# RMS norm and matmul on one core: x held in two buffers of sixteen tiles instead of five of eight

## The chip, the cores and the metric

The kernel runs on one core of a Trainium2 chip. The metric is the device time of one execution in microseconds; of several executions the median is given. One execution was also recorded by the hardware profiler, and all lines in profile fences come from that record or from questions put to its trace.

## The reference

x has 16 x 1024 rows of 512 numbers. Each row is divided by the root of the mean of its squares, scaled by gamma, and multiplied by a 512 x 768 weight matrix, all in float32:

```python
rms = np.sqrt(np.mean(x ** 2, axis=-1, keepdims=True) + eps)
x_norm = x / rms * gamma
return np.matmul(x_norm, weight).astype(np.float32)
```

x is 33.6 MB, the output 50.3 MB, the weights 1.6 MB.

## The kernel before

The 16384 rows are 128 tiles of 128 rows. Two tiles make a pair, and the main loop runs over the pairs j = 2 to 63; the first four tiles are written out by hand before it. Gamma is folded into the weights once, and the division by the root is left to the end, as a factor of each output row.

A tile goes through these steps. A DMA from SP's queue loads x (`load`, L82). GpSimd (POOL) casts a pair to bf16 (`cast`, L93, into `xb`, four buffers). ACT squares each tile with a sum along the row (`square`, L97, which also reads x) and takes the root (L101); DVE takes the reciprocal (L103). TensorE (PE) transposes the cast pair in four pieces, two bf16 numbers at a time as one float32 word (L120, into `tp`), and DVE moves the pair from PSUM to SBUF (`evac`, L127, into `xT`). Eight matmuls a tile follow (L155, into an accumulator `ops`, three buffers). ACT finishes the even tiles (L137) and DVE the odd ones (L139), each into the output buffer `ot`, and SP's queue stores it (`store`, L152).

The order of every engine's instructions is that of the program text. In iteration j POOL is told to cast pair j+3, ACT to square pair j+1, and a feeder puts the four transposes of pair j+2 between the matmuls of pair j. Since POOL has nothing else to do, it casts as soon as an `xb` buffer is free, which is when PE has transposed the pair four before.

x lies in SBUF in groups of G = 8 tiles, each in one of five buffers of 16 KB per partition. The first group is loaded in pieces of 1, 2, 1, 2 and 2 tiles, the second in two of 4, and each later group by one DMA of 2 MB in which a partition takes eight rows that lie together. Before the loop the loads of tiles 0 to 31 are issued (`load_until(AHEAD)`, with the weights between the first three tiles and the rest). In iteration j, `load_until(2 * j + AHEAD)` with AHEAD = 28 issues each group whose first tile is under 2j + 28; a group's buffer is that of the group five before.

The output lies in groups of eight tiles as well, in three buffers of 24 KB per partition. A group's store is issued after its last tile; the first group and the last two are stored in pieces.

All loads of x and all stores go through SP, which issues them in the order of the program and waits before each for its data or its buffer.

Of the kernel before, what the change touches and what calls it, by code (L numbers as in the profile page):

```python
# [12 lines left out]
F32 = mybir.dt.float32  # L13
BF16 = mybir.dt.bfloat16
AF = mybir.ActivationFunctionType
# [3 lines left out]
def kernel(  # L19
# [8 lines left out]
    nc = tc.nc  # L28
    P = 128

    x = x.flatten_outer_dims()
    out = out.flatten_outer_dims()
    N, D = x.shape
    _, O = out.shape
    K = D // P
    NT = N // P
    NP = NT // 2
    G = 8
    NG = NT // G
    AHEAD = 28  # L40
    WIDE = 512

    def stretches(parts):
        first, size, i = {}, {}, 0
        for g in range(NG):
            for n in parts.get(g, [G]):
                for t in range(i, i + n):  # L50
                    first[t], size[t] = i, n
                i += n
        return first, size

    opening = [1, 2, 1, 2, 2]
    x_first, x_size = stretches({0: opening, 1: [4, 4]})
    o_first, o_size = stretches({0: opening, NG - 2: [4, 4], NG - 1: [2, 2, 2, 1, 1]})

    def rows(ap, i, n):
        if i < G:  # L60
            return ap[i * P:(i + n) * P, :].rearrange("(p t) d -> p t d", t=n)
        return ap.rearrange("(g p t) d -> g p t d", p=P, t=G)[i // G, :, i % G:i % G + n, :]

    singles = ctx.enter_context(tc.tile_pool(name="singles", bufs=1))
    xin = ctx.enter_context(tc.tile_pool(name="xin", bufs=5))
    xbp = ctx.enter_context(tc.tile_pool(name="xb", bufs=4))
    junk = ctx.enter_context(tc.tile_pool(name="junk", bufs=2))
    stats = ctx.enter_context(tc.tile_pool(name="stats", bufs=4))
# [3 lines left out]
    outp = ctx.enter_context(tc.tile_pool(name="out", bufs=3))  # L72

    x_tiles, xb_tiles, tp_tiles, rstd_of, xT_tiles, o_tiles = {}, {}, {}, {}, {}, {}

    def held(tiles, i, n=1):
        return tiles[i // G][:, i % G:i % G + n, :]

    def load(i):
        if i // G not in x_tiles:  # L80
            x_tiles[i // G] = xin.tile([P, G, D], F32, name="xt")
        nc.sync.dma_start(out=held(x_tiles, i, x_size[i]), in_=rows(x, i, x_size[i]))  # L82

    starts = [i for i in range(NT) if x_first[i] == i]

    def load_until(i):
        while starts and starts[0] < i:
            load(starts.pop(0))

    def cast(i, engine, n=1):  # L90
        if i // 2 not in xb_tiles:
            xb_tiles[i // 2] = xbp.tile([P, 2, D], BF16, name="xb")
        engine.tensor_copy(out=xb_tiles[i // 2][:, i % 2:i % 2 + n, :], in_=held(x_tiles, i, n))  # L93

    def square(i, ssq):
        jk = junk.tile([P, D], BF16, name="jk")
        nc.scalar.activation(out=jk, in_=held(x_tiles, i)[:, 0, :], func=AF.Square, accum_out=ssq)  # L97

    def root(i, n, ssq):
        rms = stats.tile([P, 4], F32, name="rms")  # L100
# [29 lines left out]
    def transpose_tile(i):  # L130
        for h in range(2):
            transpose_word(i // 2, i % 2, h)
        evac(i // 2, i % 2, 1)

    def scale(engine, dst, src, r):
        if engine is nc.scalar:
            nc.scalar.mul(out=dst, in_=src, mul=r)  # L137
        else:
            nc.vector.tensor_single_scalar(out=dst, in_=src, scalar=r, op=mybir.AluOpType.mult)  # L139

    def accumulator():
        return opsum.tile([P, 2, WIDE], F32, name="ops").rearrange("p a b -> p (a b)")

    def out_tile(i):
        if i // G not in o_tiles:
            o_tiles[i // G] = outp.tile([P, G, O], F32, name="ot")
        return o_tiles[i // G][:, i % G, :]

    def store(i):
        first, n = o_first[i], o_size[i]  # L150
        if i == first + n - 1:
            nc.sync.dma_start(out=rows(out, first, n), in_=held(o_tiles, first, n))  # L152

    def matmul(i, k, acc, lo, hi):
        nc.tensor.matmul(out=acc[:, lo:hi], lhsT=xT_tiles[i // 2][:, i % 2, k // 2, :, k % 2], rhs=w_bf[:, k, lo:hi],  # L155
# [3 lines left out]
    def matmuls(i, acc, ks, feed=None):  # L159
        for k in ks:  # L160
            matmul(i, k, acc, 0, WIDE)
            if feed:
                feed()
            matmul(i, k, acc, WIDE, O)
# [20 lines left out]
    with tc.manual_schedule():  # L185
        g_row = singles.tile([2, P, 2], F32)
        nc.scalar.dma_start(out=g_row, in_=gamma.rearrange("(h w c) -> h w c", w=P, c=2))

        wv = weight.rearrange("(h w c) o -> w h (c o)", w=P, c=2)
        touched = singles.tile([P, 2, 1], F32)  # L190
        nc.scalar.dma_start(out=touched, in_=wv[:, :, 0:1])
        nc.scalar.preload_act_table(AF.Sqrt)  # L192
        load_until(3)
        w_f32 = singles.tile([P, K, O], F32)
        for h in range(2):
            nc.sync.dma_start(out=w_f32[:, 2 * h:2 * h + 2, :].rearrange("p c o -> p (c o)"), in_=wv[:, h, :])
        load_until(AHEAD)


        warm = singles.tile([P, WIDE], BF16)  # L200
        nc.vector.memset(warm, 0.0)  # L201
        eps_sb = singles.tile([P, 1], F32)
        nc.vector.memset(eps_sb, float(eps))  # L203
        ident_f = singles.tile([P, P], F32)
        make_identity(nc, ident_f)
        spare = accumulator()

        def warm_up(n):
            for _ in range(n):
                nc.tensor.matmul(out=spare[:, :WIDE], lhsT=warm[:, :P], rhs=warm, start=True, stop=True)  # L210

        w_bf = singles.tile([P, K, O], BF16)

        def weights(k, engine, lo=0, hi=O):
            scale(engine, w_bf[:, k, lo:hi], w_f32[:, k, lo:hi], g_sb[:, k % 2, k // 2:k // 2 + 1])


        ssq = stats.tile([P, 4], F32, name="ssq")
        warm_up(6)
        cast(0, nc.vector)  # L220
        square(0, ssq[:, 0:1])
        gp = tpsum.tile([P, 2, 2], F32, name="tp")
        for c in range(2):
            nc.tensor.transpose(out=gp[:, c, :], in_=g_row[:, :, c], identity=ident_f[:2, :2])  # L224
        g_sb = singles.tile([P, 2, 2], F32)
        nc.vector.tensor_copy(out=g_sb, in_=gp)  # L226
        transpose_tile(0)
        warm_up(3)
        cast(1, nc.vector)
        cast(2, nc.gpsimd)  # L230
        square(1, ssq[:, 1:2])
        square(2, ssq[:, 2:3])
        transpose_tile(1)
        transpose_tile(2)
        warm_up(2)

        acc = [accumulator() for _ in range(4)]
        weights(0, nc.vector, 0, WIDE)
        weights(0, nc.vector, WIDE, O)
        weights(1, nc.scalar)  # L240
        for k in (0, 1):
            for i in range(3):
                matmuls(i, acc[i], [k])
        root(0, 3, ssq)
        weights(2, nc.vector)
        weights(3, nc.scalar)
        cast(3, nc.gpsimd)
        matmuls(0, acc[0], [2, 3])
        finish_tile(0, acc[0], nc.scalar)
        transpose_tile(3)  # L250
        norms(3, 1)
        matmuls(1, acc[1], [2, 3])
        finish_tile(1, acc[1], nc.vector)
        cast(4, nc.gpsimd)
        cast(5, nc.gpsimd)
        matmuls(2, acc[2], [2, 3])
        finish_tile(2, acc[2], nc.scalar)
        matmuls(3, acc[3], [0, 1, 2, 3], feeder([2], [0, 2, 2, 0], alone=True))
        finish_tile(3, acc[3], nc.vector)
        cast(6, nc.gpsimd, 2)  # L260
        cast(8, nc.gpsimd, 2)
        norms(4, 2)


        one, two, both = [1, 1, 0, 1, 1, 0, 0, 0], [1, 0, 1, 0, 1, 0, 1, 0], [1, 1, 1, 1, 1, 1, 1, 1]
        for j in range(2, NP):
            load_until(2 * j + AHEAD)
            if j + 3 < NP:
                cast(2 * j + 6, nc.gpsimd, 2)
            if j + 1 < NP:  # L270
                norms(2 * j + 2, 2)
            if j == NP - 1:
                break
            if j < 4:
                feed = feeder([j + 1], one)
            elif j == 4:
                feed = feeder([5, 6], both)
            elif j + 2 < NP:
                feed = feeder([j + 2], two)
            else:  # L280
                feed = None
            for i, engine in ((2 * j, nc.scalar), (2 * j + 1, nc.vector)):
                a = accumulator()
                matmuls(i, a, range(K), feed)
                finish_tile(i, a, engine)


        for i in (NT - 2, NT - 1):
            for lo, hi, engine in ((0, WIDE, nc.scalar), (WIDE, O, nc.vector)):
                a = accumulator()  # L290
                for k in range(K):
                    matmul(i, k, a, lo, hi)
                scale(engine, out_tile(i)[:, lo:hi], a[:, lo:hi], rstd_of[i])
            store(i)
# [35 lines left out]
```

## Time and profile before

| | |
|---|---|
| median of 12 runs | 211.21 us (210.99 to 211.59) |
| the profiled execution's own time | 211.21 us |
| its span in the profile | 209.4 us |
| bytes moved by DMA | 85.69 MB, mean 409 GB/s |
| x loads: whole groups, issue to landing | 14 of 2048 KB, median 24.6 us |
| stores: whole groups, issue to landing | 13 of 3072 KB, median 20.1 us |
| granted clock of TensorE, mean | 0.992 |

The span begins with the first recorded instruction and ends with the last; about 1.8 us of the execution's time lie around it. PE is the TensorE matmul, DVE is VectorE, ACT is ScalarE, POOL is GpSimd, SP the engine that issues the DMAs here. In a row of slices each digit is the busy share of a fortieth of the span in tenths. In a row of a group stand the line, the engine, the operation, what it writes and reads with the shape, how often, then its busy time and the mean of one in ns, and last the engine's idle time before it and what ended most of that. "Landing" is the time from the issue of a DMA to its last completion.

### The profile page before, as it was taken

Reading aid. Unit: us, or ns where it says so; the run is one execution under the profiler, and the core shown is the slowest. Engines: PE = TensorE matmul, PEld = TensorE weight load, DVE = VectorE, ACT = ScalarE, POOL = GpSimd, SP = SyncE. Lnnn points to the kernel's source line nnn. Section 1 sums busy time; section 2 is a strip of 40 time slices with the busy share of each in tenths; the row PEclk is TensorE's granted clock in tenths of the full one; section 3 lists DMA queues with packets and bytes.
Section 4 is the critical chain, followed back from the end, with each engine's and each line's share of the span. In section 5 each row is a group of like instructions: output and inputs, shape, how many; then the busy total and the mean of one; then the engine's idle time right before and its main releaser. Section 6 shows DMA issues by size and latency. Waiting matters only on the chain.

```text
span 209.4 us, 3580 instructions
## 1 busy us (share of the span) xinstructions
PE 199.6 (95%) x1293; PEld 137.4 (66%) x1293; DVE 111.7 (53%) x204; ACT 158.2 (76%) x388; POOL 66.3 (32%) x71
## 2 busy tenths in 40 slices
PE   7799999999999999999999999999999999999960
PEld 3466766776667766776666766677666776667630
DVE  2565664465456545644654565466456545644630
ACT  4599788778777877887787778778777877887830
POOL 1156443233233323332332333233323323310000
PEclk9999999999999999999999999999999999999996
DMA  6999999999999999999999999999999999998983
GB/s 220 406 430 438 376 406 412 429 448 408 437 441 412 440 415 441 412 438 429 418 448 407 443 408 444 435 415 438 412 448 424 419 444 421 418 432 366 396 363 135
DMA packets 7206, 85.69 MB, mean 409 GB/s; under 512 B 1042, under 2 KB 1044, under 8 KB 3220
## 3 DMA queue, kind: packets, MB, share of 16 engines
q1 hardware_dynamic: 6912, 85.46, 97.0%
q8 instruction: 10, 0.16, 0.3%
q10 hardware_dynamic: 276, 0.00, 0.1%
q14 instruction: 8, 0.07, 0.1%
HBM read 35.13 MB, written 50.33 MB: 408 GB/s over the span
## 4 chain that ended last, share of the span: by engine, by line
PE 91%; DMA 3%; DVE 1%; ACT 1%; SPq 0%; issue 0%; DVEq 0%
PE ops L155 78%; PE tp L120 13%; DMA w_f<-in_weight_dram 3%; DVE ot L139 1%; ACT ot L137 0%; SPq L82 0%; ACT jk L97 0%; DVE w_bf L139 0%; DVE xT L127 0%; ACT rms L101 0%; DVE rstd L103 0%; DVEq L139 0%
## 5 line engine op out<-in xcount | busy, mean ns | idle before, releaser
L155 PE MATMUL ops<-w_bf,xT 128*128 128x256 bf16 (+1 forms) x1024 | 194.1, 326 | 0.9 <-DVE w_bf L139 0.8
L155 PEld LDWEIGHTS <-xT 128*128 128x128 bf16 x1024 | 100.2, 98 | 57.2 <-issue 1.3
L93 POOL CAST xb<-xt 128x1024 bf16<-128x1024 f32 (+1 forms) x65 | 65.6, 1014 | 118.8 <-PE tp L120 104.0
L127 DVE COPY xT<-tp 128x1024 bf16<-128x1024 bf16 (+1 forms) x67 | 44.5, 667 | 80.7 <-PE tp L120 80.7
L137 ACT ACTIVATE ot<-ops,rstd 128x768 f32<-128x768 f32 (+1 forms) x65 | 58.1, 894 | 37.7 <-PE ops L155 36.9
L97 ACT ACTIVATE jk<-xt 128x512 bf16<-128x512 f32 x128 | 78.8, 618 | 1.2 <-DMA xt<-in_x_dram 1.2
L120 PE MATMUL tp<-ident_f,xb 128*128 128x128 f32 x256 | 68.9, 274 | 0.6 <-DVE xb L93 0.6
L139 DVE TENSOR_SCALAR ot<-ops,rstd 128x768 f32<-128x768 f32 (+1 forms) x65 | 64.5, 992 | 2.9 <-PE ops L155 2.8
L120 PEld LDWEIGHTS tp<-ident_f,xb 128*128 128x128 f32 x256 | 35.8, 141 | 4.2 <-issue 1.0
L97 ACT ACTIVATION_READ_ACCUMULATOR jk<-xt 128x1 f32 x128 | 24.3, 190 | 0.0
L101 ACT ACTIVATE rms<-ssq,eps_sb 128x2 f32<-128x2 f32 (+1 forms) x64 | 18.9, 295 | 2.1
L103 DVE RECIPROCAL rstd<-rms 128x2 f32<-128x2 f32 (+1 forms) x64 | 9.9, 155 | 3.2 <-ACT rms L101 3.2
L210 PE MATMUL ops<-warm 128*128 128x512 bf16 x11 | 4.1, 514 | 1.2 <-DVE eps_sb L203 1.2
L137 ACT ACTIVATE w_bf<-w_f,g_sb 128x768 bf16<-128x768 f32 x2 | 1.9, 936 | 1.8 <-DMA w_f<-in_weight_dram 1.8
L210 PEld LDWEIGHTS <-warm 128*128 128x128 bf16 x11 | 1.3, 123 | 2.5 <-DVE eps_sb L203 1.2
L192 ACT ACT_TABLE_LOAD x1 | 1.3, 1283 | 1.7 <-issue 1.7
L93 DVE CAST xb<-xt 128x512 bf16<-128x512 f32 x2 | 1.1, 556 | 2.2 <-DMA xt<-in_x_dram 2.2
L139 DVE TENSOR_SCALAR w_bf<-w_f,g_sb 128x512 bf16<-128x512 f32 (+2 forms) x3 | 1.4, 485 | 0.7 <-DMA w_f<-in_weight_dram 0.7
L224 PEld LDWEIGHTS tp<-ident_f,g_row 2*128 2x128 f32 x2 | 0.3, 200 | 0.8 <-issue 0.8
L201 DVE MEMSET warm<- 128x256 uint32 x1 | 0.3, 272 | 0.9 <-PEq L311 0.9
L226 DVE COPY g_sb<-tp 128x4 f32<-128x4 f32 x1 | 0.2, 160 | 0.6 <-PE tp L224 0.6
L224 PE MATMUL tp<-ident_f,g_row 2*128 2x2 f32 x2 | 0.4, 264 | 0.0
(7 smaller groups left out, 1.0 us busy)
## 6 DMA issues: line engine op xcount, KB each, us to landing
out_dram<-ot SPq DMA_DIRECT2D x13, 3072.0 KB, 20.1
xt<-in_x_dram SPq DMA_DIRECT2D x14, 2048.0 KB, 24.6
out_dram<-ot SPq DMA_DIRECT2D x6, 768.0 KB, 7.2
out_dram<-ot SPq DMA_DIRECT2D x2, 1536.0 KB, 9.4
xt<-in_x_dram SPq DMA_DIRECT2D x2, 1024.0 KB, 11.4
xt<-in_x_dram SPq DMA_DIRECT2D x3, 512.0 KB, 5.8
w_f<-in_weight_dram SPq DMA_DIRECT2D x2, 768.0 KB, 6.3
out_dram<-ot SPq DMA_DIRECT2D x4, 384.0 KB, 18.0
```

What stands on the lines that cost most here:

```text
L93: engine.tensor_copy(out=xb_tiles[i // 2][:, i % 2:i % 2 + n, :], in_=held(x_tiles, i, n))
L97: nc.scalar.activation(out=jk, in_=held(x_tiles, i)[:, 0, :], func=AF.Square, accum_out=ssq)
L101: nc.scalar.activation(out=rms[:, :n], in_=ssq[:, :n], func=AF.Sqrt, scale=1.0 / D, bias=eps_sb)
L103: nc.vector.reciprocal(out=rstd[:, :n], in_=rms[:, :n])
L120: nc.tensor.transpose(out=tp_tiles[j][:, t, h, :], in_=words[:, lo:lo + P], identity=ident_f)
L127: nc.vector.tensor_copy(out=dst[:, t:t + n, :], in_=src[:, t:t + n, :])
L137: nc.scalar.mul(out=dst, in_=src, mul=r)
L139: nc.vector.tensor_single_scalar(out=dst, in_=src, scalar=r, op=mybir.AluOpType.mult)
L155: nc.tensor.matmul(out=acc[:, lo:hi], lhsT=xT_tiles[i // 2][:, i % 2, k // 2, :, k % 2], rhs=w_bf[:, k, lo:hi], start=(k == 0), stop=(k == ...
L192: nc.scalar.preload_act_table(AF.Sqrt)
L210: nc.tensor.matmul(out=spare[:, :WIDE], lhsT=warm[:, :P], rhs=warm, start=True, stop=True)
L224: nc.tensor.transpose(out=gp[:, c, :], in_=g_row[:, :, c], identity=ident_f[:2, :2])
```

## The change

x lies in groups of 16 tiles, in two buffers of 32 KB per partition. The first group is loaded in pieces of 1, 2, 1, 2, 2, 4 and 4 tiles, and each of the other seven groups by one DMA of 4 MB in which a partition takes sixteen rows that lie together. Before the loop the first two groups, tiles 0 to 31, are issued; the third and later ones in the loop with AHEAD = 20, that is two tiles before the end of the group whose buffer they take. The output stays in groups of eight tiles with the same three buffers; its rows follow the new placing of x, and the store of tiles 8 to 15 becomes two of four tiles each. The work of POOL, ACT, DVE and PE and its order stay as they are.

```diff
-    G = 8
-    NG = NT // G
-    AHEAD = 28
+    XG, OG = 16, 8
+    AHEAD = 20
...
-    x_first, x_size = stretches({0: opening, 1: [4, 4]})
-    o_first, o_size = stretches({0: opening, NG - 2: [4, 4], NG - 1: [2, 2, 2, 1, 1]})
+    last = NT // OG - 1
+    x_first, x_size = stretches(XG, {0: opening + [4, 4]})
+    o_first, o_size = stretches(OG, {0: opening, 1: [4, 4], last - 1: [4, 4], last: [2, 2, 2, 1, 1]})
 
     def rows(ap, i, n):
-        if i < G:
+        if i < XG:
             return ap[i * P:(i + n) * P, :].rearrange("(p t) d -> p t d", t=n)
-        return ap.rearrange("(g p t) d -> g p t d", p=P, t=G)[i // G, :, i % G:i % G + n, :]
+        return ap.rearrange("(g p t) d -> g p t d", p=P, t=XG)[i // XG, :, i % XG:i % XG + n, :]
...
-    xin = ctx.enter_context(tc.tile_pool(name="xin", bufs=5))
+    xin = ctx.enter_context(tc.tile_pool(name="xin", bufs=2))
...
-        if i // G not in x_tiles:
-            x_tiles[i // G] = xin.tile([P, G, D], F32, name="xt")
-        nc.sync.dma_start(out=held(x_tiles, i, x_size[i]), in_=rows(x, i, x_size[i]))
+        if i // XG not in x_tiles:
+            x_tiles[i // XG] = xin.tile([P, XG, D], F32, name="xt")
+        nc.sync.dma_start(out=held(x_tiles, XG, i, x_size[i]), in_=rows(x, i, x_size[i]))
...
-        load_until(AHEAD)
+        load_until(2 * XG)
```

The helpers `stretches` and `held` take the size of the group as an argument, and the places that call them pass XG for x and OG for the output.

More of the change, by code (lines that the diff above doesn't have):

```diff
@@ L37, with stretches @@
     NP = NT // 2
-    G = 8
-    NG = NT // G
-    AHEAD = 28
+    XG, OG = 16, 8
+    AHEAD = 20
     WIDE = 512
-    def stretches(parts):
+    def stretches(group, parts):
         first, size, i = {}, {}, 0
-        for g in range(NG):
-            for n in parts.get(g, [G]):
+        for g in range(NT // group):
+            for n in parts.get(g, [group]):
                 for t in range(i, i + n):
@@ L74, with held @@
     x_tiles, xb_tiles, tp_tiles, rstd_of, xT_tiles, o_tiles = {}, {}, {}, {}, {}, {}
-    def held(tiles, i, n=1):
-        return tiles[i // G][:, i % G:i % G + n, :]
+    def held(tiles, group, i, n=1):
+        return tiles[i // group][:, i % group:i % group + n, :]
     def load(i):
-        if i // G not in x_tiles:
-            x_tiles[i // G] = xin.tile([P, G, D], F32, name="xt")
-        nc.sync.dma_start(out=held(x_tiles, i, x_size[i]), in_=rows(x, i, x_size[i]))
+        if i // XG not in x_tiles:
+            x_tiles[i // XG] = xin.tile([P, XG, D], F32, name="xt")
+        nc.sync.dma_start(out=held(x_tiles, XG, i, x_size[i]), in_=rows(x, i, x_size[i]))
     starts = [i for i in range(NT) if x_first[i] == i]
@@ L92, in cast @@
             xb_tiles[i // 2] = xbp.tile([P, 2, D], BF16, name="xb")
-        engine.tensor_copy(out=xb_tiles[i // 2][:, i % 2:i % 2 + n, :], in_=held(x_tiles, i, n))
+        engine.tensor_copy(out=xb_tiles[i // 2][:, i % 2:i % 2 + n, :], in_=held(x_tiles, XG, i, n))
     def square(i, ssq):
         jk = junk.tile([P, D], BF16, name="jk")
-        nc.scalar.activation(out=jk, in_=held(x_tiles, i)[:, 0, :], func=AF.Square, accum_out=ssq)
+        nc.scalar.activation(out=jk, in_=held(x_tiles, XG, i)[:, 0, :], func=AF.Square, accum_out=ssq)
     def root(i, n, ssq):
@@ L144, in out_tile @@
     def out_tile(i):
-        if i // G not in o_tiles:
-            o_tiles[i // G] = outp.tile([P, G, O], F32, name="ot")
-        return o_tiles[i // G][:, i % G, :]
+        if i // OG not in o_tiles:
+            o_tiles[i // OG] = outp.tile([P, OG, O], F32, name="ot")
+        return o_tiles[i // OG][:, i % OG, :]
     def store(i):
@@ L151, in store @@
         if i == first + n - 1:
-            nc.sync.dma_start(out=rows(out, first, n), in_=held(o_tiles, first, n))
+            nc.sync.dma_start(out=rows(out, first, n), in_=held(o_tiles, OG, first, n))
     def matmul(i, k, acc, lo, hi):
```

## The prediction

> **What bounds the kernel now.** I read the busy table first, then the slices, the groups with their waits, and last the single DMAs with their landings.
>
> ```profile
> PE 199.6 (95%) x1293; PEld 137.4 (66%) x1293; DVE 111.7 (53%) x204; ACT 158.2 (76%) x388; POOL 66.3 (32%) x71
> ...
> PE   7799999999999999999999999999999999999960
> ...
> DMA  6999999999999999999999999999999999998983
> ...
> q1 hardware_dynamic: 6912, 85.46, 97.0%
> ...
> L155 PE MATMUL ops<-w_bf,xT 128*128 128x256 bf16 (+1 forms) x1024 | 194.1, 326 | 0.9 <-DVE w_bf L139 0.8
> ```
>
> Two things are full at once. PE is busy from the second slice to the end, and the matmul group lost only 0.9 us to waits. DMA queue 1 is busy 97% of the span. A pair of tiles takes PE 3.04 us (a pair's first transposes start at 27.11 and, eight pairs on, at 51.41), so eight pairs take 24.3 us and need 4.19 MB of x and 6.29 MB of out: 431 GB/s.
>
> What the queue gives is read from two loads of one 8-tile group each, and its end from the last store (second column: number of DMAs):
>
> ```profile
> L82 SPq DMA_DIRECT2D xt<-in_x_dram x2: 659/752/844, 47.0 to 59.1; - x2
> DMA to landing us min/median/max: 24.2/24.3/24.3
> ...
> L82 SPq DMA_DIRECT2D xt<-in_x_dram x1: 817/817/817, 144.2 to 144.2; - x1
> DMA to landing us min/median/max: 25.8/25.8/25.8
> ...
> L152 SPq DMA_DIRECT2D out_dram<-ot x1: 332/332/332, 202.9 to 202.9; - x1
> DMA to landing us min/median/max: 5.5/5.5/5.5
> ```
>
> From the landing at 71.2 (47.0+24.2) to 170.0 (144.2+25.8), 41.9 MB passed: 425 GB/s, slightly under PE's 431. So the queue keeps a backlog of some 20 us and it grows slowly; prefetched x hides it. At the end the last store, 0.39 MB, takes 5.5 us. On an empty queue it would take some 2.9 (the first x load, 0.26 MB, landed in 2.5[...]). So about 2.6 us of the end is DMA backlog: **PE late by up to some 2 us in the middle is forgiven at the end, and beyond that costs one for one.**
>
> [...]POOL starts tile 16 only at 23.57, when all of tiles 16 to 23 are in (5.5+17.9=23.4). [...]the granted clock is still 1.00 in 202.5 to 205.9 with no matmul running, and 0.50 in 206 to 209.
>
> **The change, part by part.**
>
> *Opening.* The same DMAs up to tile 15; then one of 4.19 MB for tiles 16 to 31 in place of two of 2.10. This is where I expect the cost.
>
> ```profile
> 23.57 3.01 POOL L93 CAST xb<-xt 128x1024 bf16<-128x1024 f32 x3 [4.06 <-DMA xt<-in_x_dram]
> ...
> 27.11 0.27 PE L120 MATMUL tp<-ident_f,xb 128*128 128x128 f32 x1
> ...
> L82 SPq DMA_DIRECT2D xt<-in_x_dram x1: 328/328/328, 7.3 to 7.3; - x1
> DMA to landing us min/median/max: 22.1/22.1/22.1
> ```
>
> The first line is POOL waiting 4.06 us for tiles 16 to 23, then casting three pairs. The second is PE's first transpose of tile 16 (pair 8 is transposed inside the matmuls of pair 6). The third is the load of tiles 24 to 31: it lands at 7.3+22.1=29.4. The new single load has the same bytes ahead of it and ends with the same byte, so tile 16 is usable at about 29.4, not 23.4. Lower bound: from tiles 12 to 15 (5.1+12.2=17.3), 4.19 MB at 425 GB/s give 27.2; the trace has a lull there (366 GB/s in 24 to 30, 431 in 18 to 24) that need not come back. Upper bound 30. I take 29.2, near the measured value. Then POOL starts 0.15 later (23.4 to 23.57), casts for 1.04, and PE starts at 30.45. **PE stalls 30.45-27.11=3.3 us** (1.3 to 4.1 by the bounds). Behind the transpose, in PE's order, stand pair 6's matmuls, and ACT and DVE wait for their accumulators. The cover before was 3.5 us, from 23.57 to 27.11 less the cast. PE has no idle time to win it back.
>
> *Reload.* The load of a 16-tile group G stands at pair 8G-9, after the store at the end of pair 8G-13 on SP. It waits for ACT's squares of tile 16G-17, done near the start of pair 8G-10, that is six us later than that store; before, a load left 0.4 us after its store. While SP waits here only the next store is queued behind it, two pairs later: nothing is held. POOL's casts of that buffer are earlier still. Does the queue run dry meanwhile? For G=2 the load leaves at about 28.5. Ahead of it are 9.96 MB of opening loads (landing 29.2) and stores of twelve tiles, 4.7 MB or 11 us; so no. It ends at 29.2+11.1+9.9=50.2; PE needs it 1.3 us before 51.4+3.3, at 53.4: margin 3.2. For G=3 the load leaves at about 54.7 (27.1, eight pairs, the stall), behind the stores of tiles 12 to 23 (3.7 and 7.4 us), and lands at 50.2+11.1+9.9=71.2; needed at 53.4+24.3=77.7. The backlog found by each later load is some 4 us and grows 0.37 a period (10.49 MB: 24.67 us at 425 GB/s against 24.3). All reloads cost 0; their cover is that backlog and 3 to 7 us of margin. Out buffers: a store lands within 17 us by the same count, the buffer is wanted after 24.
>
> *Issue and packets.* 48 DMAs on SP become 42 (x 21 to 14, out 25 to 26, two of weights). [...] It counts only if DMA sets the end; here it doesn't: 0. Splitting the store of tiles 8 to 15 in two: 0.33 us more of SP, which waits 162.7 us for DVE from 28 on. [...]
>
> *End.* The last six tiles' stores took from 202.5 (the store at 195.4 landing after 7.2) to 208.4, 5.9 us. With PE 3.3 late, the first of these leaves at 198.8+3.3=202.1[...]. Sum: **+1.6 us**; 3.3 paid in the opening, 1.7 taken back from the tail's backlog. The profiled execution took 211.21 (span 209.4 and 1.8 around it), exactly the median of the runs: 212.8.
>
> **Rivals.**
>
> 1. *Faster: no stall worth the name, DMA sets the end.* The point that decides is tile 16 usable by 27.4, for a stall of 1.5 or less. Then the tail absorbs it[...]. For it: the lull and the lower bound of 27.2. Against: the measured 29.4. With a stall near 2 the two cancel: no change.
> 2. *Clock lost.* [...]1.7 more, 214.5. For it: the drop at the end. [...]
> 3. *Reloads late too.* If a 4 MB load met the backlog of today (24.3 landing, plus 4.9 for the second half: 29.2) in the 22.7 us from issue to cast, it would be 6.5 late once; after that the delayed PE lets the queue catch up. With the tail's 1.7 off: 216. For it: landings of 24 us. Against: the count above, since with fewer loads ahead the queue is shorter.
> 4. *The change doesn't do what it says*: SP held so that the load leaves later than the buffer is free. The order of stores excludes more than 1 us; inside rival 3's margin.
>
> **How the numbers follow.** Main case 0.64 (stall 2.5 to 3.8: 212.0 to 213.3); rival 2 0.09; rival 3 0.10; rival 1 0.08, and 0.07 for the cancelling case; 0.02 for other losses. The range 211.2 to 214.7 leaves out rival 3 and rival 1. Measurement of this kernel tells 0.2% (0.42 us) from no change. Faster 0.08, same 0.07, slower 0.85.
>
> **What would show it.** Right: POOL's cast of pair 8 near 29.3, after a DMA wait of about 10 us; one PE wait of about 3 us on POOL near 27.1, as the only large one; transposes 3.3 us later from there on; last store landing about 3.9 us after issue, not 5.5; 14 x loads, 6048 packets. Wrong: cast of pair 8 before 27, PE waits on POOL near every sixteenth tile, DMA slices of 7 or less in the middle, or PEclk under 9 near slice 7.

## The result, and the profile after

The changed kernel takes 214.65 us in the median of 12 executions (212.48 to 215.97), the kernel before 211.23 (49 executions). The ratio of the two kernels is 1.0122, with a 95% interval of 1.01 to 1.0144: slower by 1.2%. The executions of the changed kernel fall in two groups, five from 212.48 to 213.43 and seven from 214.49 to 215.97, and the median falls in the upper one, so that the medians alone would give 1.016. The ratio leaves out the execution of 215.97 us, which counts as slow. The profiled one took 213.34 us (span 211.5) and belongs to the lower group.

The page of the changed kernel: the slices of PE, its granted clock and DMA, the queue, and the matmul group (line numbers are one higher than before).

```profile
PE   7699989999999999999999999999999999999990
...
PEclk9889999999999999999999999999999999999999
DMA  6999999999999899999999999999999999699885
...
q1 hardware_dynamic: 6048, 85.46, 96.2%
...
L156 PE MATMUL ops<-w_bf,xT 128*128 128x256 bf16 (+1 forms) x1024 | 195.8, 328 | 2.0 <-DVE w_bf L140 1.9
...
xt<-in_x_dram SPq DMA_DIRECT2D x7, 4096.0 KB, 17.7
```

After the opening PE is full to the end as before, and the seven loads of 4 MB land in 17.7 us in the median. DMA dips only in the last six slices (699885), when the last of x is in. The difference that matters is in the opening. In the timeline of the changed kernel (start, duration, engine, line; in brackets the idle time before it and its releaser):

```profile
29.70 1.04 POOL L94 CAST xb<-xt 128x1024 bf16<-128x1024 f32 x1 [9.23 <-DMA xt<-in_x_dram]
...
30.79 0.33 PE L121 MATMUL tp<-ident_f,xb 128*128 128x128 f32 x1 [0.86 <-POOL xb L94]
```

POOL waits 9.2 us for the 4 MB load, which was issued at 5.9 and landed 23.6 later, at 29.5. PE's first transpose of tile 16 comes at 30.79, where it came at 27.11 before: 3.7 us later. This point, which PE can't pass before the one load is in and its first pair cast, is called the gate below. PE stood still for only 0.86 of that, because its opening was already late in this execution: the weights landed 1 us later, and the clock was halved from 9.2 to 12.6. The gate at 30.8 hides that lateness; it is the gate that sets the time. The delay of 3.7 us goes through to the end, where part comes back: the last store of the changed kernel leaves at 207.0 instead of 202.9 and lands sooner after it.

```profile
L153 SPq DMA_DIRECT2D out_dram<-ot x1: 332/332/332, 207.0 to 207.0; - x1
DMA to landing us min/median/max: 3.4/3.4/3.4
```

3.4 us instead of 5.5: the store finds little or nothing ahead of it in the queue (it takes the same 3.4 in a trace below in which it leaves 6.6 later than before). It leaves 4.1 later: 3.7 of PE's, and 0.4 between DVE's last piece of output (done at 206.57, before at 202.83) and the issue on SP, whose cause stays open. It lands 2.0 later, as the spans differ (211.5 against 209.4). That accounts for the lower group. The upper group needs another cause.

### The profile page after: what moved, and what is told of

Same layout as the page of the kernel before. It is cut to its first block, busy times and chain, and to the rows that moved or that the text cites. A ratio compares the mean times of both kernels' runs of the same rounds, so it can differ in the third digit from the quotient of the medians.

```text
span 211.5 us, 3576 instructions
## 1 busy us (share of the span) xinstructions
PE 202.0 (95%) x1293; PEld 138.0 (65%) x1293; DVE 111.6 (53%) x204; ACT 158.2 (75%) x388; POOL 65.8 (31%) x71
## 3 DMA queue, kind: packets, MB, share of 16 engines
q1 hardware_dynamic: 6048, 85.46, 96.2%
## 4 chain that ended last, share of the span: by engine, by line
PE 83%; DMA 13%; POOL 0%; SPq 0%; ACTq 0%; DVE 0%; issue 0%; POOLq 0%
PE ops L156 71%; PE tp L121 12%; DMA xt<-in_x_dram 11%; DMA touched<-in_weight_dram 2%; POOL xb L94 0%; SPq L83 0%; ACTq L188 0%; DVE ot L140 0%; POOLq L94 0%
## 5 line engine op out<-in xcount | busy, mean ns | idle before, releaser
L211 PE MATMUL ops<-warm 128*128 128x512 bf16 x11 | 4.7, 574 | 1.2 <-DVE eps_sb L204 1.2
## 6 DMA issues: line engine op xcount, KB each, us to landing
xt<-in_x_dram SPq DMA_DIRECT2D x7, 4096.0 KB, 17.7
```

## Experiments

My theory: one stall in the opening, because tile 16 waits for the last byte of tile 31, and in some executions a halved clock behind that stall. The rivals: the reloads of 4 MB come late or let the queue run dry; the size or number of the buffers costs in itself.

### The changed kernel again (e1_after_again)

No edit.

> The changed kernel once more, unaltered, for more executions and a second trace. Theory (one stall in the opening while PE waits for the single 4 MB load, and in some executions the clock halved behind it): two groups of times again, near 212.7 and near 214.8, the upper group with a mean granted clock lower by about 0.005 or more. Rival (the reloads come late, or the queue runs dry in the middle): times spread with no tie to the clock, and PE waits near other sixteenth tiles.

Measured 214.97 us (214.32 to 215.82), ratio 1.0175 (1.0149 to 1.02). All five executions are in the upper group, so that of the two groups expected only one appears, and the trace shows one of them, the longest (215.82). First the granted clock from its page and a line of its PE timeline, then five stretches (length; busy us of PE, PEld, which is PE's load of weights, DVE, ACT and POOL with their instructions; PEclk; DMA share; GB/s):

```profile
PEclk9999976999999999999999999999999999999999
...
30.70 0.48 PE L121 MATMUL tp<-ident_f,xb 128*128 128x128 f32 x1 [3.74 <-POOL xb L94]
```

```profile
22.37:25.78 3.41, 3.41 (x25) 2.45 (x24) 1.91 (x4) 2.57 (x7) 0.00 (x0) 1.00 1.18 432
25.78:29.19 3.41, 1.18 (x8) 0.57 (x6) 1.69 (x3) 1.90 (x6) 0.00 (x0) 1.00 0.79 325
29.19:32.60 3.41, 1.90 (x7) 1.19 (x8) 0.00 (x0) 0.00 (x0) 3.00 (x4) 0.50 1.01 419
32.60:36.01 3.41, 3.19 (x12) 1.84 (x12) 0.32 (x1) 2.41 (x6) 1.22 (x3) 0.50 1.04 440
36.03:39.43 3.40, 3.40 (x24) 2.38 (x23) 1.89 (x4) 1.54 (x4) 1.16 (x2) 1.00 1.16 499
```

Here PE came in time and stood still for 3.74 us, to the same 30.7. The clock changes at 29.19 and at 36.0, 6.83 us apart; the stretches are half of that, so that their borders fall on the changes. In the second PE worked 1.18 of 3.41 us; from 29.19 the clock is 0.50, for two stretches. From 30.70 to the first transpose eight pairs later (57.64) it takes 26.9 us, where the kernel before takes 24.3: the clock cost 2.6. Sum: 3.6 for the gate and 2.6 for the clock, less 2.1 at the end, is 4.1; with the 0.4 ahead of the last store, as above, that is near the 4.6 by which this execution is above 211.21. The last store again lands 3.4 after its issue. PE's waits from 12 us on name POOL once, 3.7 us, so no reload stalls PE. The expected tie to the mean clock is loose: over both measurements the upper group reads 0.983 to 0.991, but two executions of the lower group read 0.989 and 0.990, the second of them the profiled one, whose clock was halved in the opening. This trace reads 0.983; nearly all others of the upper group read 0.988 to 0.991, so they may have lost the clock for one stretch and not for two, which no trace shows.

### Two loads of eight in the opening (e2_after_8_8)

```diff
-    x_first, x_size = stretches(XG, {0: opening + [4, 4]})
+    x_first, x_size = stretches(XG, {0: opening + [4, 4], 1: [8, 8]})
```

> The changed kernel with tiles 16 to 31 loaded by two DMAs of eight tiles instead of one of sixteen; buffers, reloads and all else as changed. Theory (the whole loss is the opening stall): no PE wait near 27 us, and the time is that of before or up to 0.6 us less, 210.6 to 211.3. Rival (two large buffers are short of prefetch in the steady state too, or large loads cost on the queue): 212 or more is left.

Measured 211.10 us (210.43 to 212.04) against 211.12, ratio 0.9994 (0.998 to 1.0008). In the trace of this kernel PE waits for nothing from 10 us to its last matmul. The whole loss is gone with the two large buffers, the 4 MB reloads and AHEAD = 20 still there. The rivals of the steady state fall.

### The order of two loads in the kernel before (e3_before_swap)

```diff
     starts = [i for i in range(NT) if x_first[i] == i]
+    swapped = starts.index(2 * G)
+    starts[swapped], starts[swapped + 1] = 3 * G, 2 * G
```

> The kernel before with one thing changed: of the two opening loads of groups 2 and 3 that of tiles 24 to 31 is issued first, so tile 16 is usable only when tile 31 is, at about 29.4 us; five buffers of eight tiles stay. Theory: the same stall of about 3.3 us near pair 6 and the same two groups of times as the changed kernel, 212.7 and 214.8. Rival (the size or number of the buffers, or the size of the DMAs, is the cause): 211.2.

Measured 212.56 us (211.83 to 215.42), ratio 1.0074 (1.0045 to 1.0103). Six of nine executions lie from 211.83 to 212.65, three from 214.03 to 215.42: two groups again, the lower one some 0.3 us under what I expected. In the timeline of this kernel:

```profile
29.29 3.01 POOL L95 CAST xb<-xt 128x1024 bf16<-128x1024 f32 x3 [9.33 <-DMA xt<-in_x_dram]
...
30.39 0.33 PE L122 MATMUL tp<-ident_f,xb 128*128 128x128 f32 x1 [2.62 <-POOL xb L95]
```

Five buffers and 2 MB loads do not help if tile 16 comes with the last of the 4 MB. POOL's cast began 0.4 earlier than in the changed kernel, and so did PE: 3.3 late instead of 3.7. Less the 2.1 that came back at the end of the changed kernel this gives 212.3 (211.1+3.3-2.1), the middle of the lower group. The median is under that of the changed kernel because fewer executions lie in the upper group, three of nine against twelve of seventeen.

### Work put into the stall (e4_after_fill10)

```diff
                 a = accumulator()
+                if i == 12:
+                    for _ in range(10):
+                        nc.tensor.matmul(out=a[:, :WIDE], lhsT=warm[:, :P], rhs=warm, start=True, stop=True)
                 matmuls(i, a, range(K), feed)
```

> The changed kernel with ten matmuls of zeros, 512 columns each, put ahead of tile 12's matmuls into its accumulator, which the first real matmul overwrites: 2.2 us of PE work where PE would idle. Theory (the upper group of times comes from the clock, halved after the idle stretch): the filler lies inside the stall, costs nothing, and the group near 214.8 is gone; median 212.5 to 213.2. Rival (the upper group comes from a later landing or from the queue): both groups stay and the median stays near 214.6.

Measured 213.27 us (213.18 to 213.59), ratio 1.01 (1.0078 to 1.0121). The upper group is gone and the five executions lie within 0.4 us. The median is just above the expected band, 212.5 to 213.2. In the stretch of the stall of this kernel:

```profile
28.23:31.64 3.41, 1.70 (x10) 0.86 (x9) 0.00 (x0) 0.00 (x0) 1.99 (x3) 1.00 1.01 417
```

PE is busy 1.70 of 3.41 us there and the clock stays at 1.00. PE starts tile 16 at 30.75, as in the other two traces, since the gate is the load and not PE. So some 213.3 is the time with the gate and a clock that is kept, and what the upper group has beyond it, 1 to 2.7 us, goes with the idle stretch. That each execution of the upper group lost its time to the clock is shown by one trace and by this experiment, not by a trace of each.

### PE made late by a known time (e5_before_fill7, e6_before_fill15)

The same filler in the kernel before, with seven and with fifteen matmuls:

```diff
+                if i == 12:
+                    for _ in range(7):
+                        nc.tensor.matmul(out=a[:, :WIDE], lhsT=warm[:, :P], rhs=warm, start=True, stop=True)
```

> The kernel before with seven matmuls of zeros, 512 columns each (1.5 us), ahead of tile 12's matmuls, into its accumulator, which the first real matmul overwrites; PE is late by 1.5 us from pair 6 on and never idle. Theory (the last store's 2 us of DMA backlog forgives PE a delay): 211.1 to 211.4. Rival (PE alone sets the end): 212.6.

Measured 211.20 us (210.83 to 212.33) against 211.17, ratio 0.9999 (0.9982 to 1.0015).

> The same with fifteen such matmuls, 3.2 us. Theory: 211.1+3.2-2.1=212.2, and the last store lands about 3.4 us after its issue. Rival (PE alone sets the end): 214.3. Rival (a delay this early is won back whole): 211.1.

Measured 211.99 us (211.87 to 212.72), ratio 1.0038 (1.0025 to 1.0051). From the kernel with fifteen:

```profile
L152 SPq DMA_DIRECT2D out_dram<-ot x1: 332/332/332, 206.1 to 206.1; - x1
DMA to landing us min/median/max: 3.5/3.5/3.5
```

1.5 us of delay cost nothing, 3.2 us cost 0.8, so that 2.4 are forgiven by the medians. In the recorded execution with fifteen the last store leaves 3.2 later than before and lands 1.2 later: 2.0. This is the term by which a stall is to be reduced.

### A first piece of twelve (e7_after_12_4, e10_after_12_4_again)

```diff
-    x_first, x_size = stretches(XG, {0: opening + [4, 4]})
+    x_first, x_size = stretches(XG, {0: opening + [4, 4], 1: [12, 4]})
```

> The changed kernel with tiles 16 to 31 loaded as twelve and four. Theory: the first piece is in at about 26.5 us, the cast ends at 27.7, PE waits 0.6 to 0.9 us, which the end forgives, and the clock stays: 211.0 to 211.4. Rival (a large first piece costs in proportion to its size): half of what one load of sixteen costs, 212.5 or more.

Measured 210.76 us (210.57 to 211.26) against 211.17, ratio 0.9975 (0.9964 to 0.9987), somewhat under the 211.0 to 211.4 expected.

> The changed kernel with tiles 16 to 31 loaded as twelve and four once more, unaltered, beside the one with more fillers. Theory: a ratio of 0.996 to 0.999 to the kernel before, as in the first measurement, since PE waits for nothing[...]. Rival (the first ratio was chance): 0.999 to 1.001.

Measured 210.77 us (210.58 to 211.31) against 211.09, ratio 0.9984 (0.9976 to 0.9992). In the timeline of the first of the two:

```profile
26.29 3.99 POOL L94 CAST xb<-xt 128x1024 bf16<-128x1024 f32 x4 [5.65 <-DMA xt<-in_x_dram]
```

Tile 16 is there at 26.1, and its pair's cast ends at 27.3. PE, which reached its place at 28.3 in this execution (it had waited for the weights), does not wait. In the second trace PE is not late: the cast runs from 26.04 to 27.08, PE takes tile 16 at 27.14, and no wait of PE is listed there. So a large first piece does not cost by its size, only by what it delays past PE's need. This version is the fastest here, ahead of the kernel before by 0.3 to 0.4 us in two measurements. It moves the same bytes in fewer packets (6192 against 6912: 720 fewer), but the version with eight and eight has as many packets and its interval holds no change, so the cause is not shown. What the two traces show is that the gain lies in the queue and not on PE: the last store lands at 208.0 in both (204.1+3.9 and 203.3+4.7), 0.4 earlier than before, though it leaves 1.2 and 0.4 later.

### More fillers in the opening (e9_after_12_4_warm6)

```diff
-        warm_up(2)
+        warm_up(6)
```

(with twelve and four in the opening)

> The changed kernel with tiles 16 to 31 loaded as twelve and four, and six instead of two idle matmuls of zeros ahead of the first real ones, while the weights are on their way (0.9 us more of PE work, in a gap of 0.8 to 1.9 us). Theory (part of the spread of every kernel here is a clock halved for 3.4 us in the opening, and the end hides most of it): the highest times go, the median is that of twelve and four, 210.5 to 210.8. Rival (the fillers run past the weights and delay PE): 0.2 to 0.7 us more.

Measured 210.91 us (210.52 to 211.74), ratio 0.9991 (0.9982 to 0.9999). The highest times did not go (211.74, against 211.31 with two fillers) and the median is not lower (210.77 with two, same chip); the mean granted clocks span the same range, 0.989 to 0.998 against 0.989 to 0.999. The halved clock of an opening, as in the trace of the changed kernel (0.50 from 9.2 to 12.6), isn't worth removing here, or isn't removed this way; which of the two stays open.

### Reloads two pairs later (e8_after_8_8_late)

```diff
-    AHEAD = 20
+    AHEAD = 16
```

(with eight and eight in the opening)

> The changed kernel with tiles 16 to 31 in two loads of eight (no stall in the opening) and the reloads two pairs later (AHEAD 16 instead of 20), so that each stands behind one more 3 MB store, 7.4 us. Theory (the reloads as changed have 0 to 5 us to spare, most after the first): the reload of tiles 32 to 47 lands near 58 instead of 50.5 and PE waits about 7 us near pair 14, once; less 2 at the end, plus 1.7 to 2.6 for the clock: 217 to 219. Rival (reloads have room for a whole period, the backlog is not what covers them): 211.1.

Measured 256.55 us (255.65 to 258.64), ratio 1.2152 (1.2105 to 1.2198). Both expectations missed by far. From the page of this kernel, its PE waits (us in total, times, longest), and a stretch of SP's queue:

```profile
PE   8699999969999399963999909999279995799991
...
PEclk9799999997999889997799965999858999599998
```

```profile
PE tp L121 <- POOL xb L94: 30.7, 6, 6.7
```

```profile
65.96 0.33 SPq L153 DMA_DIRECT2D out_dram<-ot  x1
66.39 0.38 SPq L83 DMA_DIRECT2D xt<-in_x_dram  x1
78.11 18.75 SPq L153 DMA_DIRECT2D out_dram<-ot  x2
96.97 0.93 SPq L83 DMA_DIRECT2D xt<-in_x_dram  x1
```

PE stalls six times, once at each reload, 5.1 us on average, and the clock drops each time (PEclk 5 to 8). I had expected one stall, after which the delay of PE would let the queue catch up. It can't: SP issues the load behind a store that waits for PE's output, 0.4 us after that 3 MB store (65.96, 66.39), so I count for it those 7.4 us and its own 9.9 (both at the 425 GB/s of the trace of before) and 1.9 more (the first x load of before landed in 2.5 us, of which 0.26 MB take 0.6 at that rate), an estimated 19.2 in all. The first load landed in 17.9, the four after it whose landing is recorded in 19.9 to 22.2. In the first four of these stalls PE is at the place 16.7 us after the issue, and wants the data 1.1 earlier, for the cast: at 15.6. The landings of 17.9, 19.9, 21.7 and 22.2 are later than that by 2.3, 4.3, 6.1 and 6.6, and the waits are 2.4, 4.4, 6.3 and 6.7. When PE is late the next issue is late by at least as much: the loads of 66.39 and 96.97 are issued 30.6 us apart, 24.3 for eight pairs, 4.4 for the wait between them and 1.9 more, with the clock lowered. In the change as made PE wants the data some 22.5 us after the issue (the load of 55.8 by 78.3, for a transpose at 79.4), and the loads from 80 us on land in 17.3 to 18.0: some 5 us to spare. Two pairs of AHEAD and one store stand between a free reload and a loss of 45 us.

## Why the prediction was right, and where not

- **The place and the mechanism** held. The stall is where it was put, comes from the completion of one DMA, and is the whole loss (e2, e3).
- **The stall's size.** Predicted 3.3 us with tile 16 in at 29.2; measured 3.7 later at the gate, with the load in at 29.5. The discount on the measured 29.4 for a lull that "need not come back" was the wrong choice: it came back (325 GB/s in 25.78 to 29.19 of the second trace). The wait on PE of about 3 us shows in the second trace (3.74); in the first it is 0.86, because PE's own opening was late.
- **The end.** Predicted 1.7 us taken back, measured 2.1 in the profile and 2.0 to 2.4 by the filler. The last store took 3.4 us in both traces of the changed kernel and in that with the filler (e4), and 3.5 in the kernel before with fifteen (e6), where 2.9 was assumed for an empty queue, so the backlog there was 2.0 to 2.1 and not 2.6; with PE 3.7 late instead of 3.3 nearly all of it came back. An estimate from the first x load gives about the assumed time: it took 2.5 us for 0.26 MB, of which the bytes at 425 GB/s are 0.6; the other 1.9 and 0.9 for the last store's 0.39 MB make 2.8. The store as measured does not bear that out. With the same 1.9 the end of the main case comes to 202.1+5.9+1.9=209.9 against 208.4. Sum of the main case: predicted +1.6, measured +2.1 (profiled execution, and 213.27 with the filler).
- **The clock, rival 2, is the step that failed.** I gave it 0.09, an estimate of mine: the trace of before has a single drop, at its end, behind 3.4 us without a matmul, and no stretch like the stall of 3.3 us. Of the 17 executions in the two measurements twelve lie in the upper group, whose excess the second trace and the filler tie to the clock. In the second trace the 3.41 us before the drop were not free of work: PE was busy for 35% of them. PEclk under 9 near slice 7, which the prediction names as a sign of being wrong, is there in that trace (7 and 6 in slices 6 and 7). The median of 214.65 is rival 2's number (214.5), not the main case's 212.8; it is inside the range by 0.05, because the range was drawn to hold rival 2, and that is luck as much as insight: the median of the second measurement, 214.97, lies outside.
- **The reloads at no cost** held: the first lands at 31.4+19.0=50.4 (predicted 50.2), the next at 55.8+17.1=72.9 (71.2), and PE waits for neither. The first left at 31.4 and not at 28.5, since the prediction left the stall out of that issue; it landed on time all the same, as its landing was counted from what the queue still held. The cover named, backlog and margin, is real. Rival 3's arithmetic of "late once" was wrong in kind (e8): it would be late at each reload.
- **Packets**: 6048 as counted. No run separates what they are worth: with the stall gone and 720 fewer than before, one version gains nothing (eight and eight) and one 0.3 to 0.4 us (twelve and four).
- **Rival 1** (no stall, DMA sets the end, faster) fits the version with twelve and four, 210.8 against 211.1 to 211.2; what makes that one faster isn't shown.

## What to carry to other kernels

When a load is merged into a larger one, ask when its first tile is wanted, and count the bytes ahead of its last byte: the merge delays the first tile to that moment, here by 3.7 us at PE. In the opening, where nothing is prefetched yet, that was paid at once; later it cost nothing with the reload issued some 22.5 us ahead of the need and landing in 17.3 to 18.0. Place a reload by the time from its issue to PE's need, counted in PE's own steps, and set against it everything that the queue holds at that moment; two pairs of AHEAD and one store more decided over 45 us here. The stall of PE was worth its length (3.6 us in the second trace), plus the lost clock (2.6), less the DMA backlog at the end (2.1): measure the last term with a filler of known length.

## What the runs showed of the hardware that was not expected

In the second trace of the changed kernel the clock was halved after a stretch of 3.41 us in which PE was busy for 1.18 us (35%), and stayed halved for two stretches. In the opening of the changed kernel, where PE stood still for only 1.90 us (before 8.89), it was halved after a stretch with 1.51 us (44%):

```profile
5.79:9.20 3.41, 1.51 (x9) 0.82 (x9) 1.50 (x4) 1.27 (x4) 0.00 (x0) 1.00 1.00 378
9.20:12.60 3.40, 3.40 (x13) 1.67 (x12) 0.80 (x2) 1.20 (x3) 1.10 (x2) 0.50 1.06 434
```

In the kernel with the swapped order a stretch with 1.54 us (45%) left it at 1.00:

```profile
26.23:29.64 3.41, 1.54 (x11) 0.80 (x8) 1.69 (x3) 2.26 (x6) 0.35 (x1) 1.00 0.92 380
29.64:33.05 3.41, 2.61 (x17) 1.96 (x19) 0.01 (x1) 1.10 (x2) 3.41 (x4) 1.00 1.12 464
```

With the filler, 1.70 us (50%) left it too. In the kernel with eight and eight a stretch near the end, with 1.41 us (41%), left it at 1.00 for the whole next stretch, in which no matmul ran:

```profile
203.39:206.80 3.41, 1.41 (x10) 0.63 (x7) 0.97 (x2) 1.09 (x2) 0.00 (x0) 1.00 0.85 344
206.80:210.22 3.42, 0.00 (x0) 0.00 (x0) 0.00 (x0) 0.00 (x0) 0.00 (x0) 1.00 0.38 152
```

So the clock was lost where PE stood still for 1.90 us at a time, and after stretches that held work, and PE's busy share alone doesn't tell the cases apart: 44% lost it and 41% kept it. The two differ in their transposes, of which the first holds four and the second none. Here are both again with the matmuls into `ops` alone, without those into `tp` (length; busy us of PE; PEclk; DMA share; GB/s), the first from the changed kernel and the second from the one with eight and eight:

```profile
5.79:9.20 3.41, 1.14 (x5) 1.00 1.00 378
...
203.39:206.80 3.41, 1.41 (x10) 1.00 0.85 344
```

Counted so, of the stretches at full clock printed in this document those with 1.14 us (33%) and 1.18 us (35%) were followed by a halved one, and those with 1.41 us (41%) and more were not (behind the one without a matmul, 206.80 to 210.22, the trace ends). This was found afterwards and is not tested by an edit; that the transposes make the difference is not shown. At the gate the clock stayed at 1.00 where PE stood still for 0.86 us (the changed kernel), 1.66 us (its filler) and 2.62 us (the swapped order), and was halved in the one trace with 3.74 us.
